# Seven projection tiles accumulated side by side at the start of a two-layer hybrid block, and a normalization without GpSimd

## The chip, the cores and the metric

The kernel runs on one NeuronCore of a Trainium2 chip. Its engines are TensorE (PE; PEld is its weight load), VectorE (DVE), ScalarE (ACT), GpSimd (POOL) and SyncE (SP, which issues the DMAs here); each works through its own queue in order. The metric is the device time of one execution in microseconds (us).

## The reference

Two layers of a hybrid block over 1024 tokens and 256 context tokens, 1024 features, all in float32. Cut to what the change touches:

```python
for l in range(DEPTH):                                   # 2 layers
    mod = silu(c) @ w_ada[l] + b_ada[l]                  # mod_c: the same of c_ctx
    shift, scale, gate = split(mod, 3)
    h  = rms_norm(x, norm_g[l]) * (1.0 + scale) + shift
    hc = rms_norm(ctx, norm_g[l]) * (1.0 + scale_c) + shift_c
    (a_glu, a_gate, nq, nk, nv, n_gate, wq, wk, wv, w_gate, merge) = split(h @ w_in[l])
    # q and k are normalized by head; then neighbourhood attention (8 heads), window attention
    # (8 heads, 2 of keys and values) and a convolution branch, each gated and projected, merged,
    y = merge_branches(...)                              # and projected by w_o
    x = x + gate * y                                     # ctx likewise, in layer 0 only
```

## The kernel before

**Layout.** Features lie on the partitions, in KC = 8 chunks of 128. The 1280 tokens are three groups: group 0 (512 tokens), group 1 (512) and group 2 (the 256 context tokens). A float32 product is made of three matmuls per chunk: each operand is split into a high part, rounded to the matmul type by ACT, and a low part, the rest, by DVE; `hh` times `w` high, `hh` times `w` low and `hl` times `w` high are added up in PSUM.

**Modulation.** `ada_wide` (L142 to L176) multiplies `silu(c)` and `silu(c_ctx)`, two columns, by `w_ada`: sixteen loads of 512 KB from SP's queue into `w_ada_t` (six buffers), eight rows of 256 columns with 16 matmul instructions each (8 chunks, each taken as two records), and `turn` (L148) which transposes a row into columns (`ada_pt`) and adds the bias; for the scale part, `gain_cols` makes the factor g(1 + scale).

**Normalization.** A `Norm` (L237) belongs to a group. `add` squares each chunk (ACT) and sums over chunks (DVE). `steps` sums over partitions on TensorE (L258, `ss_ps`), takes the reciprocal root on DVE, makes diagonal matrices of it on POOL (L267, `diag`), broadcasts it by a matmul (L270, `sr_ps`) and copies it. Then for each chunk there are four operations on three engines:

```python
nc.vector.tensor_tensor(xt[:, k, :], xt[:, k, :], self.acc, ALU.mult)                       # L277
nc.gpsimd.tensor_scalar(xt[:, k, :], xt[:, k, :], g[:, k, ci:ci + 1], shift, ALU.mult, ALU.add)  # L278
nc.scalar.activation(hh[:, k, :], xt[:, k, :], AF.Copy)                                     # L281
nc.vector.tensor_tensor(hl[:, k, :], xt[:, k, :], f32(hh[:, k, :]), ALU.subtract)           # L282
```

(`shift` stands for `mods[l][:, k, ci:ci + 1]`.)

**Projection units.** Six units of 384 columns (a head pair's q, k and v or the window heads') are projected over ten tiles of 128 tokens: tiles 0 to 3 are group 0, 4 to 7 group 1, 8 and 9 group 2. `unit_weights` (L286) loads eight chunks of 192 KB (`ru`, five raw buffers) and splits them on ACT and DVE (`wu`, eight buffers). `project_unit` (L315) does tile after tile, in each tile 8 chunks of three matmuls (L342), then the evacuation: ACT's square and DVE's sum for the norm of heads (L351, L352), ACT's copy to `stg`, and the split of the values (ACT L369, DVE L370, `vr`); `send` (L332) stores one tile while the next is computed. Unit 0 is done before the attention of a layer; the later units and other projections are a list of filler work (`Fill`), pulled between the attention's steps by a due time for each.

**The start.** The code at L1039 to L1078 runs `ada_wide` and puts in between the loading of the tokens, the norm of group 0 and the weights of unit 0; unit 0's tiles follow, and the norm steps of groups 1 and 2 stand among them.

**End of a layer.** `output_pass` (L946) multiplies by `w_o` for a group: eight steps of 128 features with 8 chunks of three matmuls (`wo_ps`, L694) and the residual on DVE (L957, `y`). `load_w` (L643) loads each weight block in two halves of 256 KB into two raw buffers (`rf`), with the high part on ACT (L649) and the low part (L650) on POOL, for groups 1 and 2 one half of them on DVE. Group 0's output pass comes first; group 1's has the norm steps of group 0 for the next layer between its steps; group 2's those of group 1, two in each step; then comes unit 0 of the next layer with group 2's steps.

**What sets the order.** TensorE's order is written by hand (its program order is the code's). The other engines are ordered by a scheduler that starts from the order in which the code emits the work.

Of the kernel before, what the change touches and what calls it, by code (L numbers as in the profile page):

```python
# [23 lines left out]
EPS = 1e-6  # L24
# [26 lines left out]
def hybrid_block_kernel(  # L51
# [90 lines left out]
    def ada_wide(l, lc, pool):  # L142

        src = w_ada[l].rearrange("(k p) n -> p k n", p=128)
        g = const.tile([128, KC, 2], F32, tag="gcol", name=f"gcol{l}")

        def turn(j0, row):
            pt = ps_tr.tile([128, 512], F32, tag="tr", name="ada_pt")  # L148
            for j in range(2):
                nc.tensor.transpose(pt[:, 2 * j:2 * j + 2], row[:, j * 128:(j + 1) * 128], ident[0:2, 0:2])  # L150
            nc.vector.tensor_tensor(
                mods[l][:, j0:j0 + 2, :], pt[:, 0:4].rearrange("p (j c) -> p j c", c=2),
                lc["b_ada"][:, j0:j0 + 2, None].to_broadcast([128, 2, 2]), ALU.add,
            )
            if j0 >= 8:
                gain_cols(l, lc, g, j0 - 8, 2)

        last = None
        for q in range(4):
            for j0 in (2 * q, 8 + 2 * q):  # L160
                ps = mm_tile("ada_ps")
                for k0 in range(0, KC, 4):
                    w = pool.tile([128, 4, 256], F32, tag="ada", bufs=6, name="w_ada_t")
                    nc.sync.dma_start(out=w, in_=src[:, k0:k0 + 4, j0 * 128:j0 * 128 + 256])
                    for k in range(4):
                        nc.tensor.matmul(
                            ps[0:2, 0:256], lhsT=sc_t[:, k0 + k, :], rhs=w[:, k, :],
                            start=(k0 + k == 0), stop=(k0 + k == KC - 1)
                        )
                row = pool.tile([2, 256], F32, tag="ada_r", bufs=2, name="ada_row")  # L170
                nc.vector.tensor_copy(row, ps[0:2, 0:256])
                if last is not None:
                    turn(*last)
                last = (j0, row)
                yield g
        turn(*last)  # L176
# [60 lines left out]
    class Norm:  # L237


        def __init__(self, gi, pool):  # L240
            self.gi, self.pool, self.n = gi, pool, GROUPS[gi][1]
            self.acc = pool.tile([128, 512], F32, tag=("acc0", "acc1")[gi % 2], bufs=2, name="sqa")[:, 0:self.n]
# [9 lines left out]
        def steps(self, l, xt, g):  # L252
# [33 lines left out]
    def unit_weights(src, pa):  # L286

        n = src.shape[2]
        ws = []
        for k in range(KC):  # L290
            raw = pa.tile([128, UW], F32, tag="ru", bufs=RU, name="ru")
            nc.sync.dma_start(out=raw[:, 0:n], in_=src[:, k, :])
            w = pa.tile([128, 2, UW], F32R, tag="wu", bufs=WU, name="wu")
            nc.scalar.activation(w[:, 0, 0:n], raw[:, 0:n], AF.Copy)
            nc.vector.tensor_tensor(w[:, 1, 0:n], raw[:, 0:n], f32(w[:, 0, 0:n]), ALU.subtract)
            ws.append(w)
        return ws
# [981 lines left out]
```

## Time and profile before

| | |
|---|---|
| median of 3 runs (lowest, highest) | 2839.9 us (2839.2, 2841.02) |
| the profiled execution | 2840.45 us, its span 2838.6 us |
| mean granted clock of TensorE, share of full | 0.986 |
| busy: PE, PEld | 96%, 83% |
| busy: DVE, ACT, POOL | 62%, 40%, 37% |
| DMA, mean over the span | 121 GB/s, 344.20 MB |

The span is the part of the execution that the profiler records; 1.85 us lie around it. A busy share is a mean over stages with different limits, so it tells which engine is the longest but not where it idles; a window gives the same for a stretch, with the clock that was granted to TensorE in it (1.00 is 2.4 GHz, 0.50 is 1.2 GHz). A timeline row merges consecutive instructions of a kind: its length is from the first one's begin to the last one's end, and in square brackets stands the idle time ahead of it with what ended it. One matmul of float32 type can be recorded as two instructions.

### The profile page before, as it was taken

To read this page: it belongs to the slowest core of one execution; us is meant where nothing else is said; L and a number is where in the kernel's file an instruction comes from. 1 tells how busy PE (TensorE), PEld (TensorE's weight loads), DVE (VectorE), ACT (ScalarE), POOL (GpSimd) and SP (SyncE) were. 2 spreads that over 40 slices of the span, in tenths; PEclk is the share of its full clock that TensorE was granted. 3 is DMA by queue.
4 is the path that set the end of the run, shared out by engine and by line. 5 is a ranking of instruction groups with operands and counts; after the bars stand their busy time and mean duration, and the time that the engine had idled before them with its cause. 6 is when DMAs were issued, how large, how long until landed. Compare 5 with 4: busy or idle time off the path is not lost. (4 is left out here: it accounts for less than half of the span.)

```text
span 2838.6 us, 43932 instructions
## 1 busy us (share of the span) xinstructions
PE 2724.9 (96%) x15060; PEld 2365.3 (83%) x15060; DVE 1746.8 (62%) x3754; ACT 1145.8 (40%) x2524; POOL 1053.6 (37%) x1252
## 2 busy tenths in 40 slices
PE   7899999999999999999999899999999999989999
PEld 4899998988888887878877899999888788767777
DVE  4567676766699806786345456676665799361132
ACT  3366666666411214121233346655556322322221
POOL 2333464633200005265645223375434100336652
PEclk9999999999999999999999999999999999999999
DMA  7444443211234323654355355552212343263345
GB/s 240 122 142 140 129 123 95 70 55 39 89 112 134 108 86 101 201 152 135 108 175 158 113 153 146 147 143 83 77 43 75 102 137 126 83 197 112 108 116 177
DMA packets 331664, 344.20 MB, mean 121 GB/s; under 512 B 82224, under 2 KB 249264, under 8 KB 331440
## 3 DMA queue, kind: packets, MB, share of 16 engines
q1 hardware_dynamic: 314160, 313.07, 37.3%
q10 hardware_dynamic: 17280, 28.32, 2.7%
q8 instruction: 119, 1.95, 0.3%
q14 instruction: 105, 0.86, 0.1%
HBM read 250.83 MB, written 90.44 MB: 120 GB/s over the span
## 5 line engine op out<-in xcount | busy, mean ns | idle before, releaser
L694 PE MATMUL mg_ps<-hh,wf 128*128 128x512 f32 (+1 forms) x1920 | 562.6, 373 | 2.0 <-POOL wf L650 1.3
L342 PE MATMUL u_ps<-wu,hh 128*128 128x384 f32 (+2 forms) x1920 | 501.7, 344 | 11.9 <-ACT hh L281 5.2
L650 POOL TENSOR_TENSOR wf<-rf,wf 128x512 fp32r<-128x512 f32 x170 | 226.0, 1331 | 751.9 <-ACT wf L649 743.2
L694 PEld LDWEIGHTS mg_ps<-hh,wf 128*128 128x128 f32 x1920 | 347.5, 188 | 71.8 <-POOL wf L650 2.1
L588 POOL TENSOR_SCALAR p<-p,rd 128x640 f32<-128x640 f32 (+1 forms) x288 | 217.0, 754 | 393.9 <-DVE rd L586 239.2
L694 PE MATMUL mg_ps<-hl,wf 128*128 128x512 f32 (+1 forms) x960 | 358.7, 374 | 0.0
L342 PEld LDWEIGHTS u_ps<-wu,hh 128*128 128x128 f32 x1920 | 330.4, 192 | 17.1 <-ACT hh L281 6.0
L342 PE MATMUL u_ps<-wu,hl 128*128 128x384 f32 (+2 forms) x960 | 323.0, 336 | 1.0 <-DVE hl L282 0.8
L580 ACT ACTIVATE p<-p,nmx 128x641 f32<-128x641 f32 (+3 forms) x288 | 222.2, 772 | 244.9 <-DVE nmx L576 120.0
L649 ACT ACTIVATE wf<-rf 128x512 fp32r<-128x512 f32 x272 | 170.4, 627 | 360.5 <-PE pp_ps L694 163.6
L694 PE MATMUL gt_ps<-hh,wf 128*128 128x512 f32 (+1 forms) x960 | 286.2, 379 | 5.7 <-DVE mg_in L945 3.2
L694 PE MATMUL pp_ps<-ogh,wf 128*128 128x512 f32 (+1 forms) x960 | 283.8, 376 | 8.0 <-DVE mg_in L945 3.9
L598 DVE TENSOR_TENSOR pt<-tp,pt 128x640 fp32r<-128x640 f32 (+1 forms) x288 | 215.8, 749 | 104.7 <-ACT pt L597 101.6
L694 PEld LDWEIGHTS pp_ps<-ogh,wf 128*128 128x128 f32 x960 | 176.1, 190 | 47.9 <-DVE mg_in L945 6.6
L894 ACT ACTIVATE mg_t<-mg_ps 128x512 f32<-128x512 f32 (+1 forms) x120 | 66.6, 555 | 367.4 <-PE mg_ps L694 362.7
L694 PE MATMUL wo_ps<-hh,wf 128*128 128x512 f32 (+1 forms) x640 | 196.4, 389 | 18.9 <-DVE mg_in L945 7.5
L694 PEld LDWEIGHTS gt_ps<-hh,wf 128*128 128x128 f32 x960 | 175.3, 189 | 43.6 <-issue 4.9
L694 PEld LDWEIGHTS mg_ps<-hl,wf 128*128 128x128 f32 x960 | 180.6, 188 | 31.8
L594 PE MATMUL tp<-ident,p 128*128 128x128 f32 x1280 | 187.4, 273 | 15.0 <-DVE pt L598 11.1
L752 DVE SCALAR_TENSOR_TENSOR cv_out<-cv_in,lc_conv_w,cv_out 128x1024 f32<-128x1024 f32 (+1 forms) x192 | 194.1, 1011 | 0.0
L597 ACT ACTIVATE pt<-tp 128x640 fp32r<-128x640 f32 (+1 forms) x288 | 182.0, 632 | 17.2 <-PE tp L594 15.0
L594 PEld LDWEIGHTS tp<-ident,p 128*128 128x128 f32 x1280 | 153.6, 140 | 42.0 <-POOL p L588 11.1
(165 smaller groups left out, 5525.8 us busy)
## 6 DMA issues: line engine op xcount, KB each, us to landing
rf<-in_wF SPq DMA_DIRECT2D x144, 256.0 KB, 2.9
rf<-in_wO SPq DMA_DIRECT2D x80, 256.0 KB, 2.9
ru<-in_wU SPq DMA_DIRECT2D x96, 192.0 KB, 3.4
bias<-in_na_bias SPq DMA_DIRECT2D x96, 192.0 KB, 2.6
w_ada_s<-in_w_ada SPq DMA_DIRECT2D x64, 256.0 KB, 3.2
nrm<-qk_d SPq DMA_DIRECT2D x40, 320.0 KB, 4.0
rf<-in_wP SPq DMA_DIRECT2D x48, 256.0 KB, 2.7
v_d<-vr SPq DMA_DIRECT2D x80, 128.0 KB, 2.0
```

The costliest lines, as they stand in the source:

```text
L342: nc.tensor.matmul(ps[:, c0:UW], lhsT=a[:, k, off * 128:(off + 1) * 128], rhs=ws[k][:, b, c0:UW], start=(k == 0 and i == 0), stop=(k == KC ...
L580: nc.scalar.activation(self.p[:, 0:n], self.p[:, 0:n], AF.Exp, bias=m, scale=1.0 if sink is None else -1.0, accum_out=self.den)
L588: nc.gpsimd.tensor_scalar(p, p, rd, 1.0, ALU.mult, ALU.mult)
L594: nc.tensor.transpose(tp[:, c * 128:(c + 1) * 128], self.p[:, c * 128:(c + 1) * 128], ident)
L597: nc.scalar.activation(self.pt[:, 0:nch, 0, :], tv, AF.Copy)
L598: nc.vector.tensor_tensor(self.pt[:, 0:nch, 1, :], tv, f32(self.pt[:, 0:nch, 0, :]), ALU.subtract)
L649: nc.scalar.activation(w[:, 0, 0:n, :], raw[:, 0:n, :], AF.Copy)
L650: eng.tensor_tensor(w[:, 1, 0:n, :], raw[:, 0:n, :], f32(w[:, 0, 0:n, :]), ALU.subtract)
L694: nc.tensor.matmul(ps[:, 0:n], lhsT=w(k, b), rhs=a[:, k, 0:n], start=(k == 0 and i == 0), stop=(k == kn - 1 and i == 2),)
L752: nc.vector.scalar_tensor_tensor(r, a[:, k:k + n], tap, r, ALU.mult, ALU.add)
L894: nc.scalar.activation(t[:, 0:n], ps[:, 0:n], AF.Tanh, scale=0.5)
```

## The change

**Normalization, in both layers.** A chunk is now three operations on two engines. DVE takes x·g·rstd in one (L272), ACT adds the shift while it makes the high part (L273), and DVE adds the shift again and subtracts the high part in one (L274). POOL has no part in it but the diagonals.

**The start.** The tokens of group 0 are loaded first and their partition sum stands ahead of the first modulation row. The modulation rows are 512 columns wide, four instead of eight, with sixteen loads of 512 KB (two chunks by 512 columns, five buffers). Rows 0 and 8 (shift and scale of the first four chunks) come first, rows 4 and 12 between chunks. `project_unit` is taken apart into a class `Unit`; seven tiles (tiles 0 to 3 of unit 0, tiles 0 to 2 of unit 1) are begun together, each in a PSUM bank of its own, and `by_chunk(k)` does chunk k of all seven as soon as that chunk is normalized. Unit 1's weights for that phase have a buffer pair of their own (`wv`, `wu_b`). After chunk 7 unit 0 goes on at tile 4, and unit 1, later and as filler of the attention, at tile 3, for which its weights are loaded and split a second time.

```diff
-    def ada_wide(l, lc, pool):
...
+        for k in range(0, KC, 2):
+            w = pool.tile([128, 2, 512], F32, tag="ada", bufs=5, name="w_ada_t")
+            nc.sync.dma_start(out=w, in_=src[:, k:k + 2, j0 * 128:j0 * 128 + 512])
...
+    def ada_row(ws, ps, pool):
+
+        for k in range(KC):
+            nc.tensor.matmul(
+                ps[0:2, :], lhsT=sc_t[:, k, :], rhs=ws[k // 2][:, k % 2, :], start=(k == 0), stop=(k == KC - 1)
             )
...
-                nc.vector.tensor_tensor(xt[:, k, :], xt[:, k, :], self.acc, ALU.mult)
-                nc.gpsimd.tensor_scalar(
-                    xt[:, k, :], xt[:, k, :], g[:, k, ci:ci + 1], mods[l][:, k, ci:ci + 1], ALU.mult, ALU.add
+                shift = mods[l][:, k, ci:ci + 1]
+                nc.vector.scalar_tensor_tensor(xt[:, k, :], xt[:, k, :], g[:, k, ci:ci + 1], self.acc, ALU.mult, ALU.mult)
+                nc.scalar.activation(hh[:, k, :], xt[:, k, :], AF.Identity, bias=shift)
+                nc.vector.scalar_tensor_tensor(
+                    hl[:, k, :], xt[:, k, :], shift, f32(hh[:, k, :]), ALU.add, ALU.subtract
                 )
-                nc.scalar.activation(hh[:, k, :], xt[:, k, :], AF.Copy)
-                nc.vector.tensor_tensor(hl[:, k, :], xt[:, k, :], f32(hh[:, k, :]), ALU.subtract)
                 yield
...
+    def project_unit(l, u, h, pa, st, ws=None, unit=None, begin=0):
...
+        unit = unit or Unit(l, u, pa, st)
+        for t in range(begin, 10):
...
+        load_x(0, 4)
+        wa = {j: ada_load(0, j, st) for j in (0,)}
+        norm = Norm(0, st, 1)
...
+        row = ada_row(wa[0], mm_tile("ada_ps"), st)
+        wa[8] = ada_load(0, 8, st)
+        next(step)
+        ada_turn(0, lc, 0, row)
+        row = ada_row(wa[8], mm_tile("ada_ps"), st)
...
+                ws0.append(unit_chunk(wU[0, 0], k, pa))
+                ws1[k] = unit_chunk(wU[0, 1], k, pa, st)
...
+        begun = [(0, 0, m[0]), (0, 1, m[1]), (0, 2, halves[0]), (0, 3, halves[1]), (1, 0, halves[2]), (1, 1, halves[3]),
+                 (1, 2, pvb)]
+
+        def by_chunk(k):
+            next(step)
+            for u, t, ps in begun:
+                units[u].chunk(t, k, (ws0, ws1)[u][k], h, ps)
+                if k == KC - 1:
+                    units[u].out(t, ps)
+
+        by_chunk(0)
+        load_units(2, 4)
+        by_chunk(1)
+        row = ada_row(wa[4], ps_tr.tile([128, 512], F32, tag="tr", name="ada_ps"), st)
+        wa[12] = ada_load(0, 12, st)
+        by_chunk(2)
+        ada_turn(0, lc, 4, row)
...
+        row = ada_row(wa[12], ps_tr.tile([128, 512], F32, tag="tr", name="ada_ps"), st)
+        by_chunk(3)
+        ada_turn(0, lc, 12, row)
+        gain_cols(0, lc, g, 4, 4)
...
+        by_chunk(4)
...
+        by_chunk(5)
...
+        step1 = norm.steps(0, xs[1], g)
+        next(step1)
+        by_chunk(6)
+        next(step1)
+        by_chunk(7)
+        run(step1)
+        unit0 = project_unit(0, 0, h, pa, state, ws0, units[0], 4)
...
+                part = (units[1], 3) if l == 0 and i == 1 else (None, 0)
```

On TensorE at the start of the program, before (`ada_ps` is a modulation row, `ada_pt` its transposes, `u_ps` a projection tile; a row with x2 is the pair of `hh` matmuls of one chunk):

```order
L166 MATMUL ada_ps<-w_ada_t,sc_t 2x256 x16
L150 MATMUL ada_pt<-ident,ada_row 128x2 x2
...
L258 MATMUL ss_ps<-ones,sqa 128x1 x4
L166 MATMUL ada_ps<-w_ada_t,sc_t 2x256 x8
L150 MATMUL ada_pt<-ident,ada_row 128x2 x2
L270 MATMUL sr_ps<-diag,ones 128x512
...
L150 MATMUL ada_pt<-ident,ada_row 128x2 x4
L342 MATMUL u_ps<-wu,hh_418 128x384 x2
```

and now, down to the first chunk's fifth tile, which is unit 1's first:

```order
L252 MATMUL ss_ps<-ones,sqa 128x1 x4
L155 MATMUL ada_ps<-w_ada_t,sc_t 2x512 x8
L264 MATMUL sr_ps<-diag,ones 128x512
L166 MATMUL ada_pt<-ident,ada_row 128x2 x4
L155 MATMUL ada_ps<-w_ada_t,sc_t 2x512 x8
L166 MATMUL ada_pt<-ident,ada_row 128x2 x4
L339 MATMUL u_ps<-wu,hh_288 128x384 x2
L339 MATMUL u_ps<-wu,hl_289 128x384
...
L339 MATMUL u_ps<-wu_b,hh_288 128x384 x2
```

The partition sum moved from behind five modulation rows to the front, and the first projection matmul from behind all eight rows of 256 columns to behind two of 512.

On SP's queue at the start, before (`x_141`, `x_142` and `x_143` are the tokens of groups 0, 1 and 2, `ru` a chunk of a unit's weights):

```order
L164 DMA w_ada_t<-in_w_ada 128x4x256 x2
L1048 DMA x_141<-in_xT 128x2x512 x4
L164 DMA w_ada_t<-in_w_ada 128x4x256 x10
L292 DMA ru<-in_wU 128x384 x5
...
L1048 DMA x_142<-in_xT 128x4x512 x2
L1048 DMA x_143<-in_xT 128x8x256
```

and now:

```order
L1068 DMA x_141<-in_xT 128x2x512 x4
L148 DMA w_ada_t<-in_w_ada 128x2x512 x5
L287 DMA ru<-in_wU 128x384
L148 DMA w_ada_t<-in_w_ada 128x2x512 x3
L287 DMA ru<-in_wU 128x384 x3
...
L1068 DMA x_142<-in_xT 128x4x512 x2
```

Group 0's tokens moved ahead of all modulation weights, and the units' weights moved in among these.

On POOL at the end of layer 0, in the output passes of groups 1 and 2, before (`wf` is a weight split's low part, `y_13129` and `y_13130` are groups 0 and 1 on their way to layer 1):

```order
L267 TENSOR_SCALAR diag<-ident,n_rstd 128x128 x4
L650 TENSOR_TENSOR wf<-rf,wf 128x512
L278 TENSOR_SCALAR y_13129<-y_13129,gcol_15730,mod_128 128x512 x3
L650 TENSOR_TENSOR wf<-rf,wf 128x512
...
L267 TENSOR_SCALAR diag<-ident,n_rstd 128x128 x4
L650 TENSOR_TENSOR wf<-rf,wf 128x512
L278 TENSOR_SCALAR y_13130<-y_13130,gcol_15730,mod_128 128x512 x3
L650 TENSOR_TENSOR wf<-rf,wf 128x512
```

and now:

```order
L261 TENSOR_SCALAR diag<-ident,n_rstd 128x128 x4
L670 TENSOR_TENSOR wf<-rf,wf 128x512 x8
L261 TENSOR_SCALAR diag<-ident,n_rstd 128x128 x4
L670 TENSOR_TENSOR wf<-rf,wf 128x512 x5
L261 TENSOR_SCALAR diag<-ident,n_rstd 128x128 x2
```

The multiplications that stood between POOL's weight splits are gone.

## Rows read from the trace of the kernel before

**Rows 1.** Part 1 of the page: each engine, busy us, share, instructions.

```profile
PE 2724.9 (96%) x15060; PEld 2365.3 (83%) x15060; DVE 1746.8 (62%) x3754; ACT 1145.8 (40%) x2524; POOL 1053.6 (37%) x1252
```

**Rows 2.** Windows, start: length, busy PE PEld DVE ACT POOL, clock, DMA share, GB/s.

```profile
0.00:51.84 51.84, 37.62 (x155) 14.07 (x155) 21.65 (x59) 14.94 (x26) 8.85 (x13) 0.93 0.92 301
...
75.90:88.20 12.30, 8.18 (x24) 5.16 (x24) 10.35 (x15) 5.12 (x10) 7.93 (x7) 0.75 0.03 11
...
111.50:139.00 27.50, 26.62 (x155) 24.82 (x154) 13.27 (x37) 11.73 (x31) 6.02 (x7) 1.00 0.77 223
```

**Rows 3.** Timeline, start: begin, length, engine, line, operation, [idle before <- releaser].

```profile
14.56 1.15 ACT L249 ACTIVATE sq<-x 128x512 f32<-128x512 f32 x2 [0.22 <-DMA x<-in_xT]
...
16.03 5.30 PE L166 MATMUL ada_ps<-w_ada_t,sc_t 128*2 128x256 f32 x16 [4.12 <-DMA w_ada_t<-in_w_ada]
...
34.51 3.61 PE L166 MATMUL ada_ps<-w_ada_t,sc_t 128*2 128x256 f32 x16
...
51.84 0.62 PE L342 MATMUL u_ps<-wu,hh 128*128 128x384 f32 x2
```

**Rows 4.** Timeline, group 1: partition sum, first step after it, diagonal.

```profile
64.65 0.95 PE L258 MATMUL ss_ps<-ones,sqa 128*128 128x1 f32 x8
...
65.63 0.16 DVE L263 TENSOR_SCALAR n_var<-ss_ps 128x4 f32<-128x4 f32 x1 [2.36 <-PE ss_ps L258]
...
68.40 1.99 POOL L267 TENSOR_SCALAR diag<-ident,n_rstd 128x128 f32<-128x128 f32 x4 [11.17 <-DVE n_rstd L111]
```

**Rows 5.** Timeline, group 1: scalings, POOL's step, tile 4's first matmuls.

```profile
79.73 2.49 DVE L277 TENSOR_TENSOR x<-x,sqa 128x512 f32<-128x512 f32 x4
...
80.52 5.39 POOL L278 TENSOR_SCALAR x<-x,gcol,mod 128x512 f32<-128x512 f32 x4 [2.09 <-DVE x L277]
...
83.42 1.01 PE L342 MATMUL u_ps<-wu,hh 128*128 128x384 f32 x2 [3.11 <-ACT hh L281]
```

**Rows 6.** Timeline, PE: pairs of matmuls in unit 0's last tiles.

```profile
106.78 0.84 PE L342 MATMUL u_ps<-wu,hh 128*128 128x384 f32 x2
...
107.74 0.84 PE L342 MATMUL u_ps<-wu,hh 128*128 128x384 f32 x2
...
110.54 0.51 PE L342 MATMUL u_ps<-wu,hh 128*128 128x384 f32 x2
...
111.06 0.51 PE L342 MATMUL u_ps<-wu,hh 128*128 128x384 f32 x2
```

**Rows 7.** Timeline, DVE: the two operations of one tile's evacuation.

```profile
88.66 0.42 DVE L352 TENSOR_REDUCE ss<-usq 128x4 f32<-128x256 f32 x1 [0.16 <-ACT usq L351]
...
89.10 0.29 DVE L370 TENSOR_TENSOR vr<-u_ps,vr 128x128 fp32r<-128x128 f32 x1
```

**Rows 8.** Windows, end of layer 0, columns as in rows 2.

```profile
1500.00:1541.00 41.00, 37.48 (x157) 29.00 (x156) 25.47 (x43) 16.20 (x28) 21.37 (x18) 1.00 0.50 159
1541.00:1585.00 44.00, 34.14 (x206) 30.74 (x206) 26.26 (x51) 16.26 (x31) 21.39 (x19) 0.81 0.44 133
...
1604.00:1612.00 8.00, 7.68 (x35) 7.68 (x36) 1.67 (x5) 1.49 (x6) 0.00 (x0) 0.79 0.69 208
```

**Rows 9.** Waits, PE, 1500 to 1612: waiter, releaser, total, times, longest.

```profile
PE wo_ps L694 <- DVE y L957: 2.7, 1, 2.7
PE u_ps L342 <- DVE vr L370: 2.0, 1, 2.0
```

**Rows 10.** Timeline, POOL, output pass of group 2.

```profile
1555.22 4.46 POOL L278 TENSOR_SCALAR y<-y,gcol,mod 128x512 f32<-128x512 f32 x3 [2.21 <-DVE y L277]
...
1559.65 1.71 POOL L650 TENSOR_TENSOR wf<-rf,wf 128x512 fp32r<-128x512 f32 x1
```

**Rows 11.** Timeline, DVE: its halves of weight splits in that pass.

```profile
1549.81 0.69 DVE L650 TENSOR_TENSOR wf<-rf,wf 128x512 fp32r<-128x512 f32 x1
...
1578.26 0.69 DVE L650 TENSOR_TENSOR wf<-rf,wf 128x512 fp32r<-128x512 f32 x1
...
1582.54 0.69 DVE L650 TENSOR_TENSOR wf<-rf,wf 128x512 fp32r<-128x512 f32 x1 [0.67 <-ACT wf L649]
```

More of the change, by code (lines that the diff above doesn't have):

```diff
@@ L140, in load_layer_consts, with ada_load @@
         )
-    def ada_wide(l, lc, pool):
+    def ada_load(l, j0, pool):
         src = w_ada[l].rearrange("(k p) n -> p k n", p=128)
[L145 to L153, printed above, removed]
-            )
[L155 to L176, printed above, removed]
@@ L178, in ada_blocks, with ada_turn @@
+    def ada_turn(l, lc, j0, row):
+        pt = ps_tr.tile([128, 512], F32, tag="tr", name="ada_pt")
+        for j in range(4):
+            nc.tensor.transpose(pt[:, 2 * j:2 * j + 2], row[:, j * 128:(j + 1) * 128], ident[0:2, 0:2])
+        nc.vector.tensor_tensor(
+            mods[l][:, j0:j0 + 4, :], pt[:, 0:8].rearrange("p (j c) -> p j c", c=2),
+            lc["b_ada"][:, j0:j0 + 4, None].to_broadcast([128, 4, 2]), ALU.add,
+        )
     def ada_blocks(items, pool):
@@ L349, in project_unit, with out @@
+        def out(self, t, ps):
+            l, u, pa, st, na, nh = self.l, self.u, self.pa, self.st, self.na, self.nh
+            nqk = 64 * nh
+            c0 = self.first_col(t)
+            self.send()
             h0 = c0 // 64
@@ L1063, in hybrid_block_kernel @@
-        load_x(1, 2)
+        g = const.tile([128, KC, 2], F32, tag="gcol", name="gcol0")
+        load_x(0, 4)
+        wa = {j: ada_load(0, j, st) for j in (0,)}
+        norm = Norm(0, st, 1)
+        for k in range(KC):
+            norm.add(xs[0][:, k, :], k)
+        step = norm.steps(0, xs[0], g)
+        next(step)
[4 more added lines that the diff above has]
+        row = ada_row(wa[8], mm_tile("ada_ps"), st)
@@ new lines, in hybrid_block_kernel, with load_units @@
+        units = [Unit(0, u, pa, state) for u in range(2)]
+        ws0, ws1 = [], {}
+        def load_units(lo, hi):
+            for k in range(lo, hi):
+                ws0.append(unit_chunk(wU[0, 0], k, pa))
+                ws1[k] = unit_chunk(wU[0, 1], k, pa, st)
+        load_units(0, 2)
+        wa[4] = ada_load(0, 4, st)
+        ada_turn(0, lc, 8, row)
+        gain_cols(0, lc, g, 0, 4)
+        m = [mm_tile("u_ps") for _ in range(2)]
+        two = [ps_s.tile([128, 1024], F32, tag="s", name="u_ps"), ps_t.tile([128, 1024], F32, tag="t", name="u_ps")]
@@ new lines, in hybrid_block_kernel @@
+        pvb = ps_pv.tile([128, 512], F32, tag="pv", name="u_ps")
+        halves = [v[:, i:i + 512] for v in two for i in (0, 512)]
+        begun = [(0, 0, m[0]), (0, 1, m[1]), (0, 2, halves[0]), (0, 3, halves[1]), (1, 0, halves[2]), (1, 1, halves[3]),
+                 (1, 2, pvb)]
+        def by_chunk(k):
+            next(step)
+            for u, t, ps in begun:
+                units[u].chunk(t, k, (ws0, ws1)[u][k], h, ps)
+                if k == KC - 1:
+                    units[u].out(t, ps)
@@ L1064, in hybrid_block_kernel @@
+        by_chunk(4)
+        load_units(6, 7)
         load_x(2, 1)
+        by_chunk(5)
+        load_units(7, 8)
         run(lcg)
-        run(step0)
-        unit0 = project_unit(0, 0, h, pa, state, ws0)
-        for gi in (1, 2):
-            if gi == 2:
-                norms[2] = Norm(2, st)
-            for k in range(KC):
-                norms[gi].add(xs[gi][:, k, :], k)
-            step = norms[gi].steps(0, xs[gi], g)
-            advance(unit0, 2)
-            next(step)
-            advance(unit0, 1)
-            run(step)
+        norm = Norm(1, st, 1)
@@ new lines, in hybrid_block_kernel @@
+        for k in range(KC):
+            norm.add(xs[1][:, k, :], k)
+        step1 = norm.steps(0, xs[1], g)
[5 more added lines that the diff above has]
+        unit0 = project_unit(0, 0, h, pa, state, ws0, units[0], 4)
+        advance(unit0, 2)
+        norm = Norm(2, st, 1)
+        for k in range(KC):
+            norm.add(xs[2][:, k, :], k)
+        step = norm.steps(0, xs[2], g)
+        next(step)
+        advance(unit0, 1)
+        run(step)
```

132 lines of the change are left out of this document (70 added, 62 removed).

## The prediction

> **What bounds the kernel now.** I read the page's first part, then windows over the stages, then waits and timelines where a window showed TensorE idle. TensorE is busy for 96% of the span [rows 1], and from 111.5 us to the attention it has no gap to speak of [rows 2]: there a saved wait elsewhere is worth nothing, and what counts is TensorE's time lost to idleness or to its lower clock. The windows show three places with such time that the change touches. The first is the start: 51.84 us pass before the first projection matmul [rows 3], and the stage in which group 1 of the tokens is split takes 12.30 us with 8.18 us of matmuls at a mean granted clock of 0.75 [rows 2]. The second is the end of layer 0: the output pass of group 1 while group 0 is normalized (1500 to 1541 us, 37.48 busy of 41) and the pass of group 2 while group 1 is normalized (1541 to 1585 us, 34.14 busy of 44, clock 0.81). The third is the short stretch after group 2's normalization (1604 to 1612 us, clock 0.79) [rows 8]. The normalization is one function, so its edit reaches layer 1's inputs as well as layer 0's.
>
> **Comparison point at the start.** In before, tile 8 of unit 0 is done at 111.6 us, the last of its chunks standing in [rows 6]. In after, the same point comes with three tiles of unit 1 done besides. A chunk of a tile (three matmuls) takes 111.06 - 110.54 = 0.52 us at full clock and 107.74 - 106.78 = 0.96 at the lower one [rows 6]; three tiles of eight chunks are 12.5 us of filler work that the attention no longer has to find room for. So the start gains what tile 8's end stays below 111.6 + 12.5 = 124.1 us.
>
> **The start, step by step (all sums are estimates from rows).**
> Until the first projection matmul: group 0's tokens no longer stand behind two 0.5 MB loads; at the 301 GB/s of the first window [rows 2] these 1.05 MB are 3.5 us, so the last tokens, used at 14.56 in before [rows 3], come near 11.5, the squares and their sum end at about 13.7, and TensorE's first work is the sum over partitions (1.0, as L258 [rows 4]): 14.7. Now TensorE's first work waits for the tokens, where before it waited for modulation weights alone; that is a price, paid here. The first modulation row: 16 instructions of twice the columns, 2 x 3.61 at full clock [rows 3], and the like block at 16.03 took 5.30, 1.7 more, after an idle stretch; I take 8.8, to 23.5. The chain to the diagonal, 68.40 - 65.63 = 2.8 on DVE and 2.0 on POOL [rows 4], ends near 19.6 and is covered by that row. The broadcast, its copy and the transposes: to 25.6. The second row, at full clock: 7.0, to 32.6; its loads wait for buffers that the first row frees between 18 and 22 us and land before they are needed. Copy, transposes, gains: 1.6; then DVE has three scalings in front of the first low part (4 x 0.66): the first tile goes on at 36.9, where before it was 51.84.
> From there to the end of chunk 7: 7 x 8 chunks x 0.52 = 29.1, two modulation rows 14.0, transposes 1.0, the two norm matmuls 1.5: 45.6. Chunk 4 needs modulation row 12, which is turned only behind chunk 3: mod, gain, a scaling, a second unit's weight, another scaling and the low part, 2.7 us of idleness. The broadcast for group 1 waits for its diagonal, 68.40 + 1.99 - 65.63 = 4.8 us from sum to diagonal [rows 4] against 3.6 us of chunk 6; with 0.5 for a weight split that stands between them on DVE, 1.7 of idleness. Some six chunks at the lower clock behind these gaps: 6 x 0.44 = 2.7. End of chunk 7: 36.9 + 45.6 + 4.4 + 2.7 = 89.6.
> Then unit 0's tile 4 needs group 1 split, and this is where the gain of the start goes. DVE has 8 scalings and 8 low parts of about 0.66 (L277's four took 2.49 [rows 5], and the new form also reads two inputs) between 7 evacuations of a reduction and a subtraction (0.42 and 0.29 long [rows 7], each begun some 0.08 before the one ahead of it has drained: 0.54): 10.6 + 3.8 = 14.3 us from 86.9, so tile 4 ends at 101.6. TensorE has only its 4.2 us there; the like stretch cost 12.30 in before [rows 2]. Bounds: wholly one after the other with ACT's parts (0.63 for each chunk, 1.0 for each evacuation), some 28 us, 13 more; all hidden behind chunk 7, 8 less. I take DVE's own sum, since the order alternates the two kinds, as it did for POOL and DVE at 79.73 to 83.42 [rows 5]. Tile 5 with four chunks at the lower clock 5.9, tiles 6 to 8 12.5, norm matmuls 0.9: **tile 8 ends at 120.9, a gain of 3.2** (bounds by the above: -10 to +8; -6 to +8 for the range). Group 2's split, without POOL's step, hides behind tiles 7 and 8.
> The second loading of unit 1's weights, 1.5 MB with 8 casts and 8 subtractions, lies beside matmuls in a stretch where TensorE is 97% busy and the others are not [rows 2]: nothing; without that cover, 8 x 0.55 on DVE. On SP's queue five of these loads stand in front of the first stores; they wait for raw buffers that chunk 5 frees, before the stores have data.
>
> **The normalization without POOL's step.** 24 multiplications on POOL in each layer go (three took 4.46 us [rows 10], four 5.39 [rows 5]); their place is taken by nothing on POOL, DVE keeps two operations per chunk, ACT one.
> Pass of group 1: TensorE waited 2.7 us once for DVE's output step [rows 9], which stood behind four low parts that waited for ACT, and ACT for POOL. In after three scalings and three low parts stand there without that chain, about 4 us sooner: **2.7** (0 to 2.7).
> Pass of group 2: this is paced by weights with two raw buffers. POOL's half of a weight split stood behind three multiplications of 4.46 us in all and began at 1559.65 [rows 10]; the next load and cast followed it, and so did DVE's half: DVE's splits at 1549.81 and 1578.26 have four intervals between them, 28.45 us, while the undisturbed one was 4.28 [rows 11]. Four such would be 17.1, a gain of 11.3 at most. DVE's own 16 operations (10.6 us) stay, about half of them in front of a split: 5.6 each, 22.4: **6.0** (2 to 11).
> After group 2: ACT's evacuation of unit 0's tile waited among the high parts for POOL, TensorE 2.0 us for the evacuation [rows 9], and 8 us at a clock of 0.79 are 21% lost, 1.7 of matmuls: **3.7** (0 to 3.7), since the high parts now end some 4 us earlier.
> Sum: 3.2 + 2.7 + 6.0 + 3.7 = 15.6. Against the profiled execution (2840.45) 2824.9; it was 0.55 above the median of the runs, so 2824.3; I say **2825**.
>
> **Rivals.**
> The split of group 1 becomes a wall. DVE's and ACT's queues are in order, evacuations and split parts wait for each other's engines, and tile 4 ends 8 us later than above: tile 8 at 129, a loss of 5 at the start with layer 0's end unchanged: 2840 - 12.4 + 5 = 2833. For it: 12.30 us for 4.2 us of matmuls in before [rows 2]. Against: POOL, the slowest link there, is out.
> The weights bound the end of layer 0 whatever POOL does. Pass 2 gains 2, the tail 2: 2840 - 3.2 - 2.7 - 4 = 2830. For it: casts that waited for loads; against: those loads were themselves late behind POOL's split [rows 10].
> Slower: the chunk-by-chunk phase runs at the lower clock. In before the clock fell to 1.2 GHz after the 3.11 us wait at 83.42 [rows 5], with chunks of 0.96 until it rose. If DVE or ACT make each chunk wait, seven tiles of eight chunks cost 56 x 0.44 = 24.6 us more: 2825 + 24.6 - 2.7 = 2847. It decides from the point at which a chunk's feed (two scalings or low parts, two weight splits: 2.4 us on DVE) exceeds its 3.6 us of matmuls; at 2.4 it doesn't, so this is unlikely.
> This is the case that the Trainium skill warns of: "TensorE: Matmul & The Clock Gate", section "Loop structure matters more than you think", puts all features of one output tile in the inner loop and holds that a wait between the matmuls lets the engine go cold. By that rule alone the change would lose, at the time just given; the row at 83.42 shows the fall of the clock after a wait, and no row here shows seven tiles sharing one.
> The early start does not happen: loads of modulation weights and of two units' weights together come as late as before, and the first tile goes on at 45 rather than 36.9: 2833.
>
> **How the numbers follow.** Forecast 0.55; wall 0.18; weights 0.15; lower clock 0.07; late loads 0.05. The range: from 2815 (the start at +8 with the end of layer 0 at about +17) to 2836, which takes in the wall, the late loads and the weights, and leaves out the lower clock and the far ends. Under 0.2% (5.7 us, about what a measurement can tell from no change) means 2834 to 2846: faster takes 0.54 of the forecast, 0.09 of the wall, 0.13 and 0.03 of the next two, 0.79; within 0.14, which is the rest of these four; slower 0.07.
>
> **What would show it.** First projection matmul at 35 to 38 us; a wait of 2 to 3 us before chunk 4; tile 4 of unit 0 the slowest of all, ending near 102; tile 8's end under 124. At the end of layer 0 no wait of ACT for POOL, no wait for DVE's output step in group 1's pass, DVE's weight splits 5 to 6 us apart in group 2's, and none of the 2.0 us wait after group 2. It is wrong if group 2's pass keeps its length, or if the windows after 111 us show new gaps of TensorE in the attention.

## The result and the profile after

The changed kernel takes 2819.95 us (median of 5 runs, 2817.89 to 2827.97) against 2839.9; the ratio is 0.9924 (95% interval 0.9896 to 0.9953). Forecast were 2825.0 and a range of 2815 to 2836. The profiled execution took 2818.42 us with a span of 2816.6: 22.0 us less than that of before. Part 1 of its page answers to [rows 1]:

```profile
PE 2710.5 (96%) x14996; PEld 2356.8 (84%) x14996; DVE 1750.2 (62%) x3752; ACT 1150.9 (41%) x2532; POOL 995.5 (35%) x1204
```

The windows of the start, with the columns of [rows 2]. Before the first projection matmul TensorE is busy for 19.5 of 37.9 us; in the phase of the seven tiles it runs at a mean clock of 0.92, and in the stretch around tile 4 at 0.83:

```profile
0.00:37.86 37.86, 19.51 (x51) 5.45 (x51) 13.35 (x35) 10.05 (x18) 1.99 (x8) 0.97 0.81 273
37.86:90.00 52.14, 48.09 (x203) 34.17 (x204) 27.00 (x65) 17.35 (x34) 1.99 (x4) 0.92 0.46 149
90.00:121.00 31.00, 24.60 (x123) 23.72 (x122) 23.10 (x60) 15.94 (x47) 1.22 (x4) 0.83 0.25 85
```

TensorE's timeline at the start (answers to rows 3, 5 and 6). The rows are: the partition sum, the first chunk's first matmul, chunk 4, group 1's broadcast, tile 3 of unit 0 and tile 1 of unit 1 in chunk 7, the first chunk of tile 4, of tile 5 and of tile 9:

```profile
13.26 1.87 PE L252 MATMUL ss_ps<-ones,sqa 128*128 128x1 f32 x8 [13.26 <-DVE sqa L244]
...
37.86 1.01 PE L339 MATMUL u_ps<-wu,hh 128*128 128x384 f32 x2 [2.00 <-ACT hh L273]
...
72.65 0.62 PE L339 MATMUL u_ps<-wu,hh 128*128 128x384 f32 x2 [2.00 <-ACT hh L273]
...
88.08 1.13 PE L264 MATMUL sr_ps<-diag,ones 128*128 128x512 f32 x2 [1.15 <-POOL diag L261]
...
94.95 1.01 PE L339 MATMUL u_ps<-wu,hh 128*128 128x384 f32 x2 [4.19 <-DVE vr L371]
...
99.45 1.01 PE L339 MATMUL u_ps<-wu_b,hh 128*128 128x384 f32 x2 [2.21 <-DVE vr L371]
...
101.54 0.84 PE L339 MATMUL u_ps<-wu,hh 128*128 128x384 f32 x2
...
106.92 0.51 PE L339 MATMUL u_ps<-wu,hh 128*128 128x384 f32 x2
...
124.48 0.51 PE L339 MATMUL u_ps<-wu,hh 128*128 128x384 f32 x2
```

DVE's timeline over the same stretch: its first scaling of group 1, the value splits (L371) of tile 2 and of unit 1's tile 0, and the last three low parts of group 1, which end at 105.26. Between 89.87 and 105.26 DVE has one gap, of 0.51 us:

```profile
89.87 0.75 DVE L272 SCALAR_TENSOR_TENSOR x<-x,gcol,sqa 128x512 f32<-128x512 f32 x1 [1.56 <-ACT sqa L265]
...
94.61 0.28 DVE L371 TENSOR_TENSOR vr<-u_ps,vr 128x128 fp32r<-128x128 f32 x1
...
99.11 0.28 DVE L371 TENSOR_TENSOR vr<-u_ps,vr 128x128 fp32r<-128x128 f32 x1
...
103.20 2.06 DVE L274 SCALAR_TENSOR_TENSOR hl<-x,mod,hh 128x512 fp32r<-128x512 f32 x3
```

The windows of the end of layer 0 (answers to rows 8): the last 41 us of the pass of group 1, the whole pass of group 2, and the stretch behind group 2's normalization. Then TensorE's longest waits from 1490 to 1594 (rows 9), and the first and last of five weight splits of DVE (rows 11), with 25.38 us for the four intervals between them in place of 28.45:

```profile
1486.80:1527.80 41.00, 40.70 (x175) 32.17 (x175) 29.41 (x48) 18.44 (x30) 11.63 (x12) 1.00 0.57 183
1527.80:1566.80 39.00, 30.41 (x204) 28.31 (x203) 27.39 (x50) 16.48 (x30) 10.29 (x10) 0.87 0.46 139
...
1586.00:1594.00 8.00, 8.00 (x48) 8.00 (x47) 1.43 (x4) 1.66 (x6) 0.00 (x0) 1.00 0.53 165
```

```profile
PE wo_ps L714 <- ACT wf L669: 3.9, 2, 3.6
PE sr_ps L264 <- POOL diag L261: 3.0, 2, 2.7
PE wo_ps L714 <- DVE wf L670: 2.1, 2, 1.9
```

```profile
1535.12 0.69 DVE L670 TENSOR_TENSOR wf<-rf,wf 128x512 fp32r<-128x512 f32 x1
...
1560.50 0.68 DVE L670 TENSOR_TENSOR wf<-rf,wf 128x512 fp32r<-128x512 f32 x1
```

**Where the 22 us are.** I compare times of the same piece of work in both traces. A landmark is a scores matmul (`sp`) of the attention, since each kernel has 288 groups of them in the same order; where one kernel has done more filler work ahead of a landmark than the other, that work is counted from the order of TensorE's instructions and added at its time in the trace (a tile is 8 x 0.52 = 4.2 us, so three tiles are 12.5). The first landmark, of before and of after:

```profile
138.83 0.36 PE L562 MATMUL sp<-kh,qst 128*128 128x256 f32 x1
```

```profile
150.05 0.36 PE L582 MATMUL sp<-kh,qst 128*128 128x256 f32 x1
```

This landmark, the first head, is 11.2 us later with 12.5 us more work done: **1.3 gained at the start**. At the 153rd group (715.45 and 712.14, with 4.2 more done) it is 7.5: **6.2 gained in the attention of layer 0**, of which the prediction said nothing. At the first group of layer 1 (1653.89 and 1631.83, the same work done) it is 22.1: **14.6 gained between**, 12.4 of them from the start of group 1's output pass on. Layer 1 adds nothing.

### The profile page after: what moved, and what is told of

Same layout as the page of the kernel before. It is cut to its first block, busy times and chain, and to the rows that moved or that the text cites. A ratio compares the mean times of both kernels' runs of the same rounds, so it can differ in the third digit from the quotient of the medians.

```text
span 2816.6 us, 43801 instructions
## 1 busy us (share of the span) xinstructions
PE 2710.5 (96%) x14996; PEld 2356.8 (84%) x14996; DVE 1750.2 (62%) x3752; ACT 1150.9 (41%) x2532; POOL 995.5 (35%) x1204
## 3 DMA queue, kind: packets, MB, share of 16 engines
q1 hardware_dynamic: 311216, 314.64, 37.6%
## 5 line engine op out<-in xcount | busy, mean ns | idle before, releaser
L339 PE MATMUL u_ps<-wu,hh 128*128 128x384 f32 (+2 forms) x1872 | 485.7, 342 | 9.9 <-DVE vr L371 4.2
L339 PEld LDWEIGHTS u_ps<-wu,hh 128*128 128x128 f32 x1872 | 319.8, 191 | 15.2 <-DVE vr L371 4.5
L339 PE MATMUL u_ps<-wu,hl 128*128 128x384 f32 (+2 forms) x936 | 312.7, 334 | 0.6 <-DVE hl L274 0.6
```

The source lines that it names most:

```text
L339: nc.tensor.matmul(ps[:, c0:UW], lhsT=a[:, k, off * 128:(off + 1) * 128], rhs=w[:, b, c0:UW], start=(k == 0 and i == 0), stop=(k == KC - 1 ...
```

## The experiments

The times in the second column are medians; the landmarks are those of one profiled execution of each kernel, and the columns behind them give what it has gained on the profiled execution of before, worked out as above.

| kernel | us | first head at | gained there | at group 153 | at layer 1 |
|---|---|---|---|---|---|
| before | 2840 | 138.83 | | | |
| after | 2819.95 | 150.05 | 1.3 | 7.5 | 22.1 |
| after, again | 2820.25 | 150.36 | 1.0 | 7.2 | 22.2 |
| normalization alone | 2815.69 | 122.91 | 15.9 | 15.8 | 25.6 |
| normalization alone, again | 2815.73 | 125.94 | 12.9 | 12.5 | 25.2 |
| normalization in layer 0's input alone | 2826.16 | 121.62 | 17.2 | 17.4 | 19.7 |
| start alone | 2837.21 | 157.76 | -6.4 | -0.8 | 3.2 |
| three tiles ahead alone | 2831.11 | 150.63 | 0.7 | 6.5 | 9.3 |
| POOL's step on DVE | 2836.63 | 135.37 | 3.5 | 1.2 | 5.5 |
| after, splits first | 2823.55 | 150.83 | 0.5 | 5.5 | 20.3 |
| after, group 1 early | 2814.9 | 140.98 | 10.3 | 16.2 | 30.8 |
| normalization, one tile ahead | 2814.55 | 127.74 | 15.3 | 15.9 | 27.6 |
| normalization, three tiles ahead | 2807.2 | 138.97 | 12.4 | 19.8 | 36.3 |
| normalization, six tiles ahead | 2820.75 | 152.14 | 11.7 | 10.6 | 22.1 |

**The normalization alone.** The kernel before with the new lines of `steps` and nothing else of the change:

> The kernel before with only the new normalization (no POOL step), start as it was. Theory A (the gains are of three separate places: about 12 us at the end of layer 0 from the normalization, about 1 up to the first head from the new start, about 6 to 8 in the attention of layer 0 because three tiles of unit 1 are done ahead): 12 us less at the end of layer 0 and 1 to 4 less at the start where group 0 and group 1 are split without POOL, nothing in the attention, 2824 to 2828 us. Rival B (what the attention gains comes from the normalization or is scatter between runs, not from tiles done ahead): the attention is shorter here too, 2817 to 2822. Rival C (the end of layer 0 gains only because the work of before it is shifted): under 6 us there, 2833 or more.

Measured: 2815.69, ratio 0.9912 (0.9899 to 0.9925). It is faster than the whole change, so the rewritten start, taken with it, loses some 4 us (the pair run once more: 2820.25 and 2815.73). None of the three expectations had it: the attention gains nothing, as theory A said, but the first head comes 15.9 us earlier where 1 to 4 were expected, and from group 153 to layer 1 it gains 9.7.

**The start alone.** The changed kernel with the four old operations in `steps`:

> The changed kernel with the old normalization (POOL's step back) in both layers. Theory A: end of layer 0 as in the kernel before, attention 6 to 8 shorter, the way to the first head 0 to 4 longer than in the changed kernel, since a chunk's feed passes through POOL and group 1's split too: 2831 to 2837 us. Rival: the chunk-by-chunk phase doesn't live without the new normalization (each chunk waits for four operations on three engines, the clock stays low): 2845 or more. Other rival (the start needs nothing of it): 2828 to 2831.

Measured: 2837.21, ratio 0.9992 (0.9983 to 1.0). The first head is 7.7 us later than in the changed kernel, worse than the 0 to 4 of theory A; the attention gives its 5.6 all the same. So of the change's 20 us nearly all needs the normalization.

**Three tiles ahead.** In the kernel before, behind unit 0:

```diff
         run(unit0)
+        unit1 = project_unit(0, 1, h, pa, state)
+        next(unit1)
+        advance(unit1, 3)
...
+            if nm == "u1" and l == 0:
+                fill.add(nm, unit1)
+                continue
```

> The kernel before, with three tiles of unit 1 done straight behind unit 0, ahead of the attention, in place of as its filler; nothing else is changed. Theory A (tiles done ahead take away the wait of a head's transposes for q and k that had only just been projected, 2.3 and 1.8 us in before, and what follows from it): the way to the first head is 12.5 longer plus 0 to 4 for unit 1's weights, the attention 6 to 8 shorter after the 12.5 are given back: 2834 to 2838 us, and no wait of t_ps for POOL's nrm at heads 4 and 6. Rival B (scatter, or another cause): 2839 to 2844.

Measured: 2831.11, ratio 0.9959 (0.9946 to 0.9972), 3 us better than expected. The attention gains 5.8 with nothing else changed, and 2.8 more come before layer 1. The waits of TensorE in the attention of layer 0 show the cause: the transposes of a head's q and k (`t_ps`) waited for POOL's scaling of them (`nrm`), which waits for the unit's last tile to be stored and loaded again. In before, then here:

```profile
PE t_ps L388 <- POOL nrm L419: 4.1, 2, 2.3
```

```profile
PE t_ps L388 <- DVE qst L453: 1.3, 3, 0.5
```

In the changed kernel that wait is absent too. The two waits are 4.1 us, but they are not the whole account. The windows from the first head to group 153, before and here:

```profile
138.83:715.45 576.62, 560.88 (x3734) 529.20 (x3734) 404.55 (x1162) 362.29 (x880) 261.27 (x404) 1.00 0.35 99
```

```profile
150.63:713.14 562.51, 549.88 (x3680) 518.14 (x3680) 402.58 (x1157) 359.70 (x873) 260.36 (x404) 1.00 0.36 101
```

TensorE's idle time fell by 3.1 us in all (15.7 to 12.6), since other waits grew, and its busy time by 11.0, 2.7 more than the 8.3 of work that was moved out. Part of the 2.7 fits the clock, which was 0.96 around the first of the two waits (330 to 372 us) and 1.00 in the same work here (335 to 375); no run shows what the rest is.

**Group 1's splits before the evacuations.** The changed kernel with this:

```diff
-                if k == KC - 1:
-                    units[u].out(t, ps)
...
         by_chunk(7)
+        for u, t, ps in begun[0:2]:
+            units[u].out(t, ps)
         run(step1)
+        for u, t, ps in begun[2:]:
+            units[u].out(t, ps)
```

> The changed kernel with chunk 7 of the seven tiles without evacuations between; two tiles are evacuated, then group 1 is split, then the other five are evacuated. In the changed kernel TensorE waited in chunk 7 for two evacuations (4.2 and 2.2 us), each of the tile that lies in the other half of the same PSUM pair, and tile 4 began at 101.5 us. Theory A (tile 4 is held by those waits and by DVE's evacuations between the splits): chunk 7 ends near 92.5 without a wait, tile 4 ends 4 to 5 us earlier, near 102, and all of it reaches the end: 2814 to 2817 us. Rival (DVE and ACT need the time anyway, and the later evacuations hold the two PSUM buffers of tiles 4 to 6): same as the changed kernel within 1 us, 2819 to 2821.

Measured: 2823.55, ratio to before 0.9943 (0.993 to 0.9957): no gain over the changed kernel. In TensorE's timeline the first half of theory A came: tile 4 began at 92.06, had only short waits for the splits and was done at 102.1, 4.8 us earlier. But then tile 6 waits for a PSUM buffer, 3.39 us from 107.49 on, and begins at 110.88, against 111.44 in the changed kernel. DVE's row stands behind TensorE's:

```profile
94.53 0.62 PE L339 MATMUL u_ps<-wu,hh 128*128 128x384 f32 x2 [0.97 <-ACT hh L273]
...
98.50 1.01 PE L339 MATMUL u_ps<-wu,hh 128*128 128x384 f32 x2 [0.73 <-ACT hh L273]
...
110.88 0.98 PE L339 MATMUL u_ps<-wu,hh 128*128 128x384 f32 x2 [3.39 <-DVE rs_a L110]
```

```profile
107.53 0.16 DVE L257 TENSOR_SCALAR n_var<-ss_ps 128x2 f32<-128x2 f32 x1 [2.33 <-PE ss_ps L252]
```

DVE's work on group 1's splits and six of the evacuations, from 89.21 to 105.20 us, is about as long as on the splits and all seven in the changed kernel, as the rival had it. But DVE then stood idle for 2.33 us: the next operation in its queue, the first of group 2's norm, waited for TensorE's sum of group 2, and the last evacuations stood behind it. So the waits in chunk 7 alone are not what the start loses; whether this order would have gained with group 2's step placed later was not run.

**Group 1 earlier.** The changed kernel with group 1's tokens loaded ahead of chunk 2, its `Norm` and first two steps ahead of chunk 3, two splits ahead of each of chunks 4, 5 and 6, and the seven evacuations behind chunk 7:

```diff
+        load_x(1, 2)
         by_chunk(2)
...
+        norm = Norm(1, st, 1)
+        for k in range(KC):
+            norm.add(xs[1][:, k, :], k)
+        step1 = norm.steps(0, xs[1], g)
+        next(step1)
...
+        next(step1)
+        next(step1)
         by_chunk(4)
```

> The changed kernel with group 1's sum and broadcast moved ahead of chunk 3, its first six chunks split between chunks 3 and 6, and the seven evacuations behind chunk 7 in place of between its tiles. Theory A (the rewritten start loses at tile 4, where DVE's 16 operations of group 1 and seven evacuations stand in a row, 15.4 us of DVE from 89.9 on, while DVE has idle time in the chunk phase): tile 4 begins at 92 to 96 us in place of 101.5, the first head comes 6 to 10 us earlier than 150.05, 2810 to 2814 us. Rival B (DVE's work in the chunk phase then makes each chunk wait and the clock falls): first head at 149 or later, 2819 or more.

Measured: 2814.9, ratio to before 0.9903 (0.9884 to 0.9923). Tile 4 begins at 93.70 without a wait, and the stretch that had 24.6 busy us of 31 at a clock of 0.83 is full:

```profile
93.70 0.52 PE L339 MATMUL u_ps<-wu,hh 128*128 128x384 f32 x2
```

```profile
90.00:121.00 31.00, 31.00 (x182) 30.95 (x181) 21.05 (x65) 18.30 (x57) 1.23 (x4) 1.00 0.44 144
```

Theory A holds in its place: the first head is 9.1 earlier, and the median lies just above its range. The profiled execution, 2808.97, was the fastest of the six; by the medians the gain over the changed kernel is 5 us. The rewritten start lost that because DVE's work for group 1 stood in one piece behind chunk 7 while DVE was busy for only 27 us of the 52 of the chunk phase. Even so this kernel is 7.7 us slower than the old start with three tiles ahead (2807.2, below); what makes up the difference was not measured.

**POOL's step on DVE.** In the kernel before, `nc.vector.tensor_scalar` in place of `nc.gpsimd.tensor_scalar` in `steps`:

> The kernel before with L278 (times gain, plus shift) on DVE in place of POOL: still four operations for a chunk, one more on DVE, none on POOL. Theory A (what the new normalization removes is POOL's time, 1.35 us for a chunk, and the hand-over to it): most of its gain is here too, less 24 more operations on DVE at 0.4 to 0.7 us, of which those of groups 0 and 1 show: 2817 to 2826 us. Rival B (it is the number of operations in the chain, or DVE's load, that counts): 2832 or more.

Measured: 2836.63, ratio 0.9983 (0.9971 to 0.9994). My theory A falls: taking POOL out is worth 3.4 us, and leaving the operation out 21 more. The windows of the first 123 us in before, with the normalization alone, with it once more, and with the step on DVE (columns as in rows 2):

```profile
0.00:51.50 51.50, 37.41 (x152) 13.87 (x152) 21.31 (x58) 14.94 (x26) 8.51 (x13) 0.93 0.93 303
51.50:85.00 33.50, 26.58 (x125) 22.45 (x125) 24.45 (x61) 15.71 (x37) 16.79 (x16) 0.90 0.19 55
85.00:122.90 37.90, 34.95 (x167) 32.34 (x166) 21.61 (x70) 13.94 (x40) 8.55 (x13) 0.86 0.34 105
```

```profile
0.00:51.50 51.50, 36.67 (x161) 14.89 (x162) 22.77 (x63) 16.78 (x29) 2.29 (x8) 0.97 0.92 300
51.50:85.00 33.50, 30.04 (x161) 26.54 (x160) 28.06 (x81) 17.73 (x43) 3.21 (x8) 1.00 0.24 70
85.00:122.90 37.90, 37.67 (x220) 36.12 (x219) 20.91 (x57) 16.83 (x45) 5.25 (x7) 1.00 0.68 196
```

```profile
0.00:51.50 51.50, 37.83 (x158) 14.68 (x159) 22.39 (x61) 16.23 (x28) 2.29 (x8) 0.93 0.92 303
51.50:85.00 33.50, 30.32 (x148) 27.06 (x147) 27.79 (x80) 17.12 (x40) 3.23 (x8) 0.90 0.22 66
85.00:122.90 37.90, 37.61 (x218) 36.23 (x217) 19.64 (x56) 16.52 (x45) 5.23 (x6) 1.00 0.59 174
```

```profile
51.50:85.00 33.50, 27.81 (x131) 22.42 (x129) 30.09 (x78) 16.94 (x39) 1.87 (x4) 0.92 0.23 65
85.00:122.90 37.90, 36.21 (x186) 34.96 (x186) 23.74 (x80) 14.27 (x42) 1.80 (x5) 0.89 0.41 122
```

From 85 us on, where group 1's tokens are in use, both runs of the short normalization have TensorE busy for 37.6 of 37.9 us at a clock of 1.00; with four operations, on POOL or on DVE, it is 35 to 36 at 0.86 to 0.89. With the step on DVE, DVE's chunk is 0.61 + 0.46 + 0.61 = 1.68 us from start to start, with the fused ones 2 x 0.67 = 1.33; TensorE then waits again and again for a high or low part (0.3 to 0.7 us, ten times between 56 and 87 us), and its mean clock is 0.92 and 0.89 in the two windows. That the waits bring the lower clock is how I read these rows; no run takes them apart. The two executions of the short normalization warn against more: both have the same waits from 72 to 78 us, the longest of 0.97 us, and the clock fell behind it in the second alone:

```profile
76.90 0.62 PE L342 MATMUL u_ps<-wu,hh 128*128 128x384 f32 x2 [0.97 <-ACT hh L279]
```

```profile
77.42 0.93 PE L342 MATMUL u_ps<-wu,hh 128*128 128x384 f32 x2 [0.97 <-ACT hh L279]
```

**The normalization in layer 0's input alone**, the old one at the end of layer 0 (the new lines under `if l == 0`):

> The kernel before with the new normalization for layer 0's input alone; for layer 1's input, at the end of layer 0, POOL's step stays. Theory A (of the 24.6 us of the normalization alone some 15 are of the start and some 10 of the end of layer 0): first head at 122 to 126 us, end of layer 0 as in the kernel before, 2823 to 2828 us. Rival (the first head of that one profile was early by a clock that another execution doesn't get, and the start gives 8 or less): first head at 130 or later, 2831 or more.

Measured: 2826.16, ratio 0.9946 (0.9934 to 0.9958). It splits the 24.6 us of the normalization into 14.3 at the start and, by the difference to 2815.7, 10.5 at the end of layer 0, as theory A had it. The profiled execution was the fastest of the five (2822.11): its first head, 121.62, is a little ahead of the expected 122, and it gained 2.3 us behind group 153, where the old normalization still stands, so its landmarks say less than the medians.

**Both gains without the rewritten start.** The normalization alone with three, six or one tile of unit 1 ahead:

> The kernel before with the new normalization and with three tiles of unit 1 done straight behind unit 0: at the first head it has done what the changed kernel has done there, with the old start. Theory A (the two gains measured apart, 24.6 and 9.2 us, are of different places and add up; the rewritten start itself is a loss): first head at 134 to 138 us (150.05 in the changed kernel), the waits of t_ps for POOL's nrm gone, 2805 to 2809 us. Rival B (the same waits stand behind both gains): 2813 to 2817.

Measured: 2807.2, ratio 0.9878 (0.9856 to 0.99). The gains add up (0.9912 x 0.9959 = 0.9871). This version beats both kernels, 12.7 us under the changed one, with the old start. Its first head, 138.97, came a little behind the expected 134 to 138; there it has done the same work as the changed kernel 11.1 us sooner.

> As the one with three tiles, with six tiles of unit 1 done ahead. Theory A (what is needed is that a unit's last tile is stored some time before the head that reads it; three tiles give that, and more of them only move work): the same as with three within 2 us, 2804 to 2809. Rival (each tile done ahead gives some 2 us, as three gave 6): 2799 to 2803. Other rival (the filler runs out at the end of the attention and its waits show): 2811 or more.

Measured: 2820.75, ratio 0.9926 (0.9907 to 0.9946): more is worse. The attention loses 1.1 where three tiles gain 7.4, and waits come up behind it for the merge sums (`y`) and the weights, as the other rival said. TensorE's waits from 130 to 1440 us, the longest and the one on weights:

```profile
PE pp_ps L694 <- DVE y L943: 5.5, 2, 3.3
...
PE mg_ps L694 <- ACT wf L649: 2.4, 1, 2.4
```

Which of them costs most was not taken apart.

> The new normalization in the kernel before, with one tile of unit 1 done ahead in place of three. Theory A (the heads' waits need only that a unit's last tile is done some 2.3 us sooner than now; one tile of 4.2 us is enough): both waits of t_ps for POOL's nrm gone, 2806 to 2810 us, as with three. Rival (the gain grows with the tiles): one wait stays in part, 2811 to 2814.

Measured: 2814.55, ratio 0.9906 (0.9893 to 0.9919). Wrong: one tile takes nothing off. Both waits stand as they were:

```profile
333.60 0.67 PE L388 MATMUL t_ps<-ident,nrm 128*128 128x128 f32 x4 [2.36 <-POOL nrm L419]
...
415.69 0.83 PE L388 MATMUL t_ps<-ident,nrm 128*128 128x128 f32 x4 [1.75 <-POOL nrm L419]
```

In the code a unit is finished by force ahead of the head that needs it (`fill.finish`), so I suppose that a lead shorter than what is forced there moves the forced part and leaves the wait. That is not shown, and why it takes more than one tile and not more than three I did not measure.

**How far a landmark can be trusted.** The changed kernel and the normalization alone, unaltered:

> The changed kernel once more, unaltered, for how far one profile's landmarks can be trusted. If they can: first head at 148 to 152 us (150.05), head 152 at 710 to 715 (712.14), 2816 to 2824 us. If the granted clock differs from one execution to the next: first head off by 3 us or more.

> The kernel before with only the new normalization once more, unaltered. If one profile can be trusted: granted clock 1.00 from 51 to 123 us, first head at 121 to 125 us (122.91), 2812 to 2819 us. If the granted clock at the start differs from one execution to the next: first head at 126 or later with a clock under 0.97 there, and the median still near 2816 to 2820.

Measured: the changed kernel 2820.25 (ratio 0.993, 0.9917 to 0.9942) with its landmarks within 0.4 us; the normalization alone 2815.73 (0.991, 0.9898 to 0.9922), its first head 3.0 us later (125.94, just short of the 126 expected for that case), at a granted clock of 0.90 from 51.5 to 85 us where the other execution had 1.00. So a landmark of the old start holds to some 3 us, while the two medians of each kernel agree within 0.3.

## Why the prediction was right, point by point, and where it was not

The median, 2819.95, is 5 us under the forecast and inside the range. Only the end of layer 0 gained what was forecast, and there the errors of its three parts cancel. The start gained less than forecast, and the attention, which had no term, more than made up for it; that the total fell into the range is luck in that part.

- **The start.** Its steps came close one by one: first projection matmul at 36.9 (37.86), the wait before chunk 4 of 2.7 (2.00 and 0.42), the wait for the broadcast of 1.7 (1.15). DVE's sum for group 1, 14.3 us, was 15.4 (89.87 to 105.26). What failed is where that sum begins and what stands in it: it was put at 86.9, with chunk 7 done at 89.6. It began 3 us later, behind a longer chunk phase, and TensorE's own chunk 7 waited inside it, 4.19 and 2.21 us for value splits, to 101.5. Tile 4 ended at 106.9 (forecast 101.6) and tile 8 at 124.5 (120.9): the gain by then is 124.1 - 124.5, nothing, in place of 3.2. The first head has 1.3. The rival of the wall at group 1 was therefore right in kind (5.3 of the 8 us it priced), and its place is shown by the run with group 1 early. The bounds of this term hold two slips: 8 less at tile 4 is a gain of 11, not 8, and all one after the other is 26.4 us by the terms named, not 28. The run with group 1 early gained 10.3 at the first head, more than the upper bound as it was written.
- **What the small gain hides.** The 3.2 was taken as one number for the start. The runs show two large ones of opposite sign: with the old start and three tiles ahead, the normalization gives 12.4 at the first head (without the tiles 12.9 to 17.2 in single profiles, 14.3 by the medians), and the rewritten start, against the same work done in the old order, costs 11.1 of them (150.05 against 138.97). The prediction held the stretch in before with 12.30 us for 8.18 of matmuls [rows 2] against the seven tiles; three operations in place of four shorten it in the old order, with TensorE at 37.6 of 37.9 us and at full clock behind 85 us.
- **The attention.** Taken as 0, measured 6.2. The step that failed is "12.5 us of filler work that the attention no longer has to find room for": the three tiles were priced at their own length, but ahead of time they also take away waits of heads for a unit only just projected, 4.1 us that stand in the trace of before and that I did not look up since TensorE had no large gap in the windows. Not all of the gain is traced to them (3.1 us less idle time, the rest in TensorE's busy time). The seven runs with three tiles done ahead gain 5.0 to 7.4 there, the five with one or none at most 0.6.
- **The end of layer 0.** Forecast 2.7 + 6.0 + 3.7 = 12.4, measured 3.6 in the pass of group 1, 4.7 in that of group 2 and 4.1 behind it, 12.4 in all. The waits named went: none for DVE's output step, none of 2.0 us for the evacuation, none of ACT for POOL. Group 2's pass was taken too high: DVE's weight splits lie 6.35 us apart, not 5.6, and TensorE still waits there 6.0 us for weights (3.65 at 1555.67 the longest), and 2.65 for group 1's diagonal on POOL, for which the forecast had no term. Against [rows 8] the window of that pass is 5.0 us shorter, of which 1.3 are idle time and 3.7 TensorE's own busy time, at a mean clock of 0.87 in place of 0.81; so what was won there is clock more than shorter waits. The rival "weights" priced the pass at 2 in place of 6. One more raw weight buffer, which would test it, was not tried.
- **Between.** Some 2 us from the 153rd group to the output passes were not forecast. The run with three tiles ahead alone has 2.8 there, so it seems to belong to the tiles too; the mechanism stays open.
- **The clock.** The chunk phase has a mean clock of 0.92. The clock fell at the waits that ended at 37.86 and 72.65, and behind each of them three tiles' chunks took 0.88 to 0.96 us in place of 0.52 before it rose; six chunks at the lower clock is what the forecast had. Apart from chunks 0 and 4 no chunk waited for its feed, so the slower rival (2847) did not come. The Trainium skill, "TensorE: Matmul & The Clock Gate", section "Loop structure matters more than you think", shows as its bad nest one with a long DMA wait ahead of every matmul, in which TensorE goes cold. This trace agrees as far as the clock fell at the 2.0 us waits; in chunks 1 to 3, 5 and 6, without a wait for their feed, seven tiles within a chunk ran at 0.52 us each, so the order of the loops alone did not lower the clock.

The sum, 15.6 against the profiled execution, came out as 22.0; of the 6.4 between, the attention is 6.2, the start -1.9, and the way to the passes 2.1.

## What to carry to other kernels

Price the two edits of a change apart: here the small one (one operation fewer for each chunk) was worth more than the whole, and the large one lost at the start and won part of it back in a later stage. Work done ahead of its time can be worth more than its length if someone later waits for its result (three tiles here; one gave nothing and six lost the gain again); look for that wait by the tile that carries it, since windows of a busy engine hide waits of 2 us. Where a stage ended in DVE's queue, moving the waits about gained nothing here, and moving work to where DVE idled gained 5 us.

## What the runs showed of the hardware

The granted clock of TensorE in the first 51.5 us, whose instructions are the same, was 0.97 in one execution of the kernel with the normalization alone and 0.93 in the other, and 1.00 and 0.90 in the 33.5 us that followed. A first head can so come 3 us earlier or later in the same program.

A float32 operation of 128 x 512 on DVE took, from start to start, 0.46 us with one tensor and two columns (the step on DVE), 0.61 with two (L277 and L282 in that kernel) and 0.67 with two tensors and a column (L272, L274); POOL's took 1.35 to 1.49 beside them (four in 5.39 us and three in 4.46) [rows 5, 10]. I had taken the fused ones at the price of the plain ones, 0.66 against a mean of 0.62 in [rows 5], close to what they took.
